# Feed-forward gate and up as seven half products in seven of 24 chunks

## The chip, the cores and the metric

The kernel runs on one core of a Trainium2 chip. The metric is the device time of one execution in microseconds (us); the median of three runs is compared.

## The reference, cut to what matters

x is 256 tokens of 1024. Two layers each do a feed-forward, a mixer (a gated recurrence and attention) and a second feed-forward. The change touches the feed-forwards alone:

```python
def swiglu_ffn(h, w_up, w_down):            # w_up: 1024 x 5632, w_down: 2816 x 1024
    gate, up = jnp.split(h @ w_up, 2, axis=-1)
    return (jax.nn.silu(gate) * up) @ w_down
for l in range(DEPTH):                      # DEPTH = 2
    x = x + 0.5 * swiglu_ffn(rms_norm(x, g_ffn1[l]), w_up1[l], w_down1[l])
    ...                                     # the mixer
    x = x + 0.5 * swiglu_ffn(rms_norm(x, g_ffn2[l]), w_up2[l], w_down2[l])
```

## The kernel before

Each float32 product is made of three matmuls in the format fp32r: an operand is split into a high part (a cast) and a low part (what the cast lost), and high x high, high x low and low x high are added in PSUM.

**Weights.** The unit is a half chunk ("hc"): two k tiles of 128 rows by 512 columns, 0.52 MB. `plan` lists all of them in the order of use. `emit_dma` (L299) issues the next load on SP, into one of four raw buffers; `emit_hi` casts it on ScalarE (L332), `emit_lo` subtracts on VectorE (L341), and then calls `emit_dma` for the load four places on. The high and low parts lie in rings of six (`RING`): `can_hi` allows a cast when the entry six places back has been used by both token halves (`NT` = 2).

**Products.** `visit` runs one hc for one token half of 128: two k tiles, three matmuls of 512 columns each (L398 to L400). `block` runs four hcs for token half 0, then the same four for half 1, into two PSUM banks of the pools x or z (z has four). In `ffn` a chunk is 512 of the 2816 hidden columns (the sixth has 256): a gate block, an up block, and then the down block of the chunk before (four hcs). `ev_g` makes silu on ScalarE (L635), `ev_u` multiplies on VectorE (L640), and `h_chain` turns the result: a copy (L316 or L319), a transpose by a DMA on SP (L515), a copy back, and a split (L500, L502).

**The order of work.** The class `Sched` keeps a clock for each engine with planned costs while the program is written out. After each k tile, `hook` steps the waiting chains and `split` casts and subtracts ahead. So each engine's order is fixed ahead of time, and an instruction that waits holds up what is behind it on its engine. Background chains are stepped only where their engine is planned less than 2.5 us behind (`SLACK`). `rows_chain` loads the small vectors early in the first feed-forward, transposes them later, and then makes tables of ones on ScalarE (L675). Twelve equal slots of SBUF are given out and back by `slot` and `free`.

Of the kernel before, what the change touches and what calls it, by code (L numbers as in the profile page):

```python
# [15 lines left out]
P = 128  # L16
# [31 lines left out]
WARM0 = 10  # L48
WARM1 = 8


# [104 lines left out]
def act_c(n, ap=0):  # L156
    return 0.11 + 0.000833 * n + 0.093 * ap
# [7 lines left out]
def hybrid_encoder_kernel(  # L165
# [72 lines left out]

    hcs = []

    def plan(w, r0, c0, nk, ncol):
        hcs.append((w[r0:r0 + nk * P, c0:c0 + ncol].rearrange("(k p) n -> p k n", p=P), nk, ncol))

# [16 lines left out]

    def plan_ffn(wu, wd):
        for c, (f0, n) in enumerate(CH):
            plan_block(wu, f0, n)
            plan_block(wu, FF + f0, n)
# [22 lines left out]
    for l in range(L):  # L287
        plan_ffn(w_up1[l], w_down1[l])
        plan_mix(l)
        plan_ffn(w_up2[l], w_down2[l])  # L290
    NHC = len(hcs)
# [7 lines left out]
    def emit_dma(cuts=1):  # L299
        i = nxt["dma"]  # L300
        if i >= NHC:
            return
        nxt["dma"] += 1
        src, nk, ncol = hcs[i]
# [4 lines left out]
        raws[i] = t  # L309

# [12 lines left out]
    def can_hi():  # L323
        i = nxt["hi"]
        return i < NHC and i in raws and (i < RING or used[i - RING] == NT)

    def emit_hi():
        i = nxt["hi"]
        nxt["hi"] += 1
        _, nk, ncol = hcs[i]  # L330
        hi = new(whi_p, [P, nk, ncol], "whi", F32R)
        nc.scalar.copy(hi, raws[i])  # L332
        his[i] = hi, S.use("a", act_c(1024))

    def emit_lo():
        i = nxt["lo"]
        nxt["lo"] += 1
        _, nk, ncol = hcs[i]
        hi, end = his.pop(i)
        lo = new(wlo_p, [P, nk, ncol], "wlo", F32R)  # L340
        nc.vector.tensor_tensor(out=lo, in0=raws.pop(i), in1=f32(hi), op=ALU.subtract)  # L341
        S.use("d", dve_c(1024), end)
        ready[i] = (hi, lo)
        emit_dma()

    def split(lead, idle):
        if nxt["pos"] < 3:
            lead = 1
        if can_hi() and nxt["hi"] - nxt["pos"] <= lead and (idle is None or S.busy("a") < idle):
# [8 lines left out]
    def first_split(xT, gcol):  # L358


        _, nk, ncol = hcs[0]
        raw = raws.pop(0)
        hi, lo = new(whi_p, [P, nk, ncol], "whi", F32R), new(wlo_p, [P, nk, ncol], "wlo", F32R)
# [18 lines left out]
    def get_hc(i):  # L382
        while nxt["lo"] <= i:
            if nxt["hi"] == nxt["lo"]:
                assert can_hi()
                emit_hi()
            emit_lo()
        nxt["pos"] = max(nxt["pos"], i)
        return ready[i]

    def visit(i, acc, lhs, k0, tok, first, last, fin=None):

        hi, lo = get_hc(i)
        _, nk, ncol = hcs[i]
        ts = slice(tok * P, tok * P + P)
        for kk in range(nk):
# [5 lines left out]
            if kk == nk - 1:  # L402
                used[i] += 1
                if used[i] == NT:
                    ready.pop(i)
                if fin is not None:
                    fin()
# [192 lines left out]

    def ffn(nrm, nxn, mixed=0):
        lhs = nrm.lhs()
# [12 lines left out]
        def down(c, tok, hf, i0, last):  # L615
# [5 lines left out]
            for i in range(m):  # L621
# [3 lines left out]
                visit(i0 + i, dacc[tok, hf], src, 2 * i, tok, c == 0 and i == 0, last and i == m - 1, fin)  # L625

        for c, (f0, n) in enumerate(CH):
            hT[c] = slot([P, 2, 4, T], F32R)
# [600 lines left out]
    def program():  # L1229
# [39 lines left out]
        for l in range(L):  # L1269
            nx = Norm(cols[:, l, R_GM:R_GM + KD])  # L1270
            if l:
                S.add(load_fw(l), S.now, "a")
            ffn(nrm, nx, 1 if l == 0 else 0)
# [6 lines left out]
            ffn(nrm, nx)  # L1280
            nrm = nx
# [31 lines left out]
```

## Time and profile before

| | |
|---|---|
| median of three runs | 1267.83 us (1267.33 to 1272.08) |
| the profiled execution | 1271.76 us, span 1270.0 us |
| granted TensorE clock, mean | 0.999 |
| busy share of the span | TensorE 99%, VectorE 65%, ScalarE 65%, GpSimd 5% |
| matmuls | 5889 |
| DMA | 253.50 MB, mean 200 GB/s |

The profile is of one execution; times in its rows are us from the first instruction of the span. A busy time counts an engine's instructions alone; matmuls overlap, so the spacing of their starts, and not their duration, says what one costs.

### The profile page before, as it was taken

Reading aid. Unit: us, or ns where it says so; the run is one execution under the profiler, and the core shown is the slowest. Engines: PE = TensorE matmul, PEld = TensorE weight load, DVE = VectorE, ACT = ScalarE, POOL = GpSimd, SP = SyncE. Lnnn points to the kernel's source line nnn. Section 1 sums busy time; section 2 is a strip of 40 time slices with the busy share of each in tenths; the row PEclk is TensorE's granted clock in tenths of the full one; section 3 lists DMA queues with packets and bytes.
Section 4 is the critical chain, followed back from the end, with each engine's and each line's share of the span. In section 5 each row is a group of like instructions: output and inputs, shape, how many; then the busy total and the mean of one; then the engine's idle time right before and its main releaser. Section 6 shows DMA issues by size and latency. Waiting matters only on the chain.

```text
span 1270.0 us, 16219 instructions
## 1 busy us (share of the span) xinstructions
PE 1255.3 (99%) x5889; PEld 1033.6 (81%) x5889; DVE 824.9 (65%) x1158; ACT 826.8 (65%) x1086; POOL 68.6 (5%) x88
## 2 busy tenths in 40 slices
PE   9999999999999999999999999999999999999998
PEld 7887887788877888888878888878887778888887
DVE  6655556798777666555475555578987767655553
ACT  6657556886799456555566555569768984665553
POOL 4000000001400000000000000000032000000000
PEclk9999999999999999999999999999999999999999
DMA  7977769576567568667768677596676665687773
GB/s 252 247 212 217 223 173 257 142 222 208 166 174 188 178 190 212 205 213 206 193 195 238 199 207 207 157 276 163 203 218 156 184 189 174 200 223 215 215 189 102
DMA packets 212304, 253.50 MB, mean 200 GB/s; under 512 B 92488, under 2 KB 104960, under 8 KB 212224
## 3 DMA queue, kind: packets, MB, share of 16 engines
q1 hardware_dynamic: 210288, 249.21, 67.8%
q0 software_dynamic: 1920, 3.26, 1.2%
q8 instruction: 46, 0.75, 0.3%
q14 instruction: 34, 0.28, 0.1%
q10 hardware_dynamic: 16, 0.00, 0.0%
HBM read 229.88 MB, written 2.10 MB: 183 GB/s over the span
## 4 chain that ended last, share of the span: by engine, by line
PE 72%; DVE 5%; DMA 2%; issue 1%; ACT 1%; SPq 0%; DVEq 0%; ACTq 0%
PE x L398 11%; PE x L400 11%; PE x L399 11%; PE z L398 9%; PE z L400 9%; PE z L399 9%; PE y L398 3%; PE y L400 3%; PE y L399 3%; DVE wlo L341 2%; PE z L1010 1%; PE z L479 1%; PE y L1082 1%; DMA tmp<-in_b_gate_dram 1%; PE z L820 1%
## 5 line engine op out<-in xcount | busy, mean ns | idle before, releaser
L341 DVE TENSOR_TENSOR wlo<-raw,whi 128x1024 fp32r<-128x1024 f32 x423 | 510.2, 1221 | 220.6 <-ACT whi L332 213.3
L332 ACT CAST whi<-raw 128x1024 fp32r<-128x1024 f32 x423 | 439.5, 1048 | 208.4 <-PE z L400 122.0
L398 PE MATMUL x<-whi,s 128*128 128x512 f32 x800 | 323.3, 404 | 5.5 <-ACT s L500 2.4
L399 PE MATMUL x<-wlo,s 128*128 128x512 f32 x800 | 312.9, 391 | 0.8 <-DVE wlo L341 0.7
L400 PE MATMUL x<-whi,s 128*128 128x512 f32 x800 | 313.3, 392 | 0.1
L398 PE MATMUL z<-whi,s 128*128 128x512 f32 (+1 forms) x752 | 279.6, 372 | 1.0 <-ACT s L500 1.0
L399 PE MATMUL z<-wlo,s 128*128 128x512 f32 (+1 forms) x752 | 279.8, 372 | 0.1
L400 PE MATMUL z<-whi,s 128*128 128x512 f32 (+1 forms) x752 | 279.6, 372 | 0.0
L398 PEld LDWEIGHTS x<-whi,s 128*128 128x128 f32 x800 | 150.4, 188 | 40.9 <-ACT s L500 4.7
L400 PEld LDWEIGHTS x<-whi,s 128*128 128x128 f32 x800 | 150.4, 188 | 34.9 <-DVE s L502 2.5
L399 PEld LDWEIGHTS x<-wlo,s 128*128 128x128 f32 x800 | 150.6, 188 | 30.9 <-DVE wlo L341 2.0
L399 PEld LDWEIGHTS z<-wlo,s 128*128 128x128 f32 x752 | 141.8, 189 | 26.0 <-DVE wlo L341 1.8
L398 PEld LDWEIGHTS z<-whi,s 128*128 128x128 f32 x752 | 141.8, 189 | 25.6 <-ACT s L500 1.4
L400 PEld LDWEIGHTS z<-whi,s 128*128 128x128 f32 x752 | 141.8, 189 | 25.0 <-DVE s L502 0.8
L319 ACT COPY tmp<-nat 128x1024 uint16<-128x1024 uint16 (+1 forms) x88 | 96.3, 1114 | 75.9 <-DMA nat<-tmp 67.9
L398 PE MATMUL y<-whi,s 128*128 128x512 f32 x208 | 82.4, 396 | 0.0
L400 PE MATMUL y<-whi,s 128*128 128x512 f32 x208 | 81.1, 390 | 0.0
L399 PE MATMUL y<-wlo,s 128*128 128x512 f32 x208 | 81.1, 390 | 0.0
L640 DVE SCALAR_TENSOR_TENSOR nat<-z,rstd,nat 128x512 f32<-128x512 f32 (+1 forms) x48 | 33.9, 705 | 56.3 <-PE z L400 56.3
L502 DVE TENSOR_TENSOR s<-tmp,s 128x512 fp32r<-128x512 f32 (+1 forms) x71 | 46.6, 656 | 34.8 <-ACT s L500 34.4
L500 ACT CAST s<-tmp 128x512 fp32r<-128x512 f32 (+1 forms) x71 | 42.1, 594 | 28.1 <-DVE tmp L529 26.5
L635 ACT ACTIVATE nat<-z,rstd 128x512 f32<-128x512 f32 (+1 forms) x46 | 29.9, 651 | 45.1 <-PE z L400 45.0
(164 smaller groups left out, 903.1 us busy)
## 6 DMA issues: line engine op xcount, KB each, us to landing
raw<-in_w_up_dram SPq DMA_DIRECT2D x175, 512.0 KB, 4.7
raw<-in_w_in_dram SPq DMA_DIRECT2D x112, 512.0 KB, 4.6
raw<-in_w_down_dram SPq DMA_DIRECT2D x88, 512.0 KB, 4.5
raw<-in_w_lru_out_dram SPq DMA_DIRECT2D x16, 512.0 KB, 5.0
raw<-in_w_attn_out_dram SPq DMA_DIRECT2D x16, 512.0 KB, 3.8
raw<-in_w_o_dram SPq DMA_DIRECT2D x16, 512.0 KB, 4.4
s<-ones_d POOLq DMA_DIRECT2D x16, 128.0 KB, 4.3
tmp<-in_b_gate_dram SPq DMA_DIRECT2D x8, 256.0 KB, 4.7
```

Source lines behind the costliest of these rows:

```text
L319: nc.scalar.copy(out_, in_)
L332: nc.scalar.copy(hi, raws[i])
L341: nc.vector.tensor_tensor(out=lo, in0=raws.pop(i), in1=f32(hi), op=ALU.subtract)
L398: nc.tensor.matmul(acc, lhsT=lhs(0, k0 + kk)[:, ts], rhs=hi[:, kk, :], start=st, stop=False)
L399: nc.tensor.matmul(acc, lhsT=lhs(0, k0 + kk)[:, ts], rhs=lo[:, kk, :], start=False, stop=False)
L400: nc.tensor.matmul(acc, lhsT=lhs(1, k0 + kk)[:, ts], rhs=hi[:, kk, :], start=False, stop=sp)
L479: nc.tensor.transpose(dst_ps[:, j * P:(j + 1) * P], src[:, j * P:(j + 1) * P], ident)
L500: nc.scalar.copy(hi, t)
L502: nc.vector.tensor_tensor(out=lo, in0=t, in1=f32(hi), op=ALU.subtract)
L635: nc.scalar.activation(s[tok][0], acc, AF.Silu, scale=rs(tok))
L640: nc.vector.scalar_tensor_tensor(out=h, in0=acc, scalar=rs(tok), in1=h, op0=ALU.mult, op1=ALU.mult)
L820: nc.tensor.matmul(ps[:, g, :], lhsT=wax[0][:, g, n, :], rhs=xr[0][:, n, :], start=True, stop=True)
```

## The change

Seven chunks (the fourth in the first feed-forward, the third and fifth in the other three) compute gate and up together as one product of 2 x 2 blocks: tokens in halves, the 1024 rows in halves of 512, and gate and up as the two column halves. Seven products of half blocks take the place of eight. Names: "11" and "12" are the upper rows of gate and up, "21" and "22" the lower ones; t1 to t4 are sums of these, made in place: t3 = 22 - 12, t1 = 12 - 11, t2 = t3 + 11, t4 = 21 - t2. A set is seven operands of two hcs each, used in the order 11, t1, t2, 21, t3, 22, t4, each hc once (`uses` 1) and not twice. Its eight loads go to five slots and not to raw buffers; they are placed in the list behind each of the eight ordinary loads ahead of the set, and a set's hcs trigger no loads. t3 and t1 are summed by a background chain planned 6 us after the last load, t2 and t4 when the low part of what they overwrite has been made. `sums_chain` makes three sums of the token halves once a feed-forward and splits them. In `seven` the products come into z banks and are joined by seven additions on VectorE and one copy on ScalarE; gate and up of token half 0 are made behind the fourth and sixth product, those of half 1 behind the last. The wait in `rows_chain` is 25 us and not 70.

```diff
+SEVEN = ((3,), (2, 4), (2, 4), (2, 4))
+    ORDER = ("11", "t1", "t2", "21", "t3", "22", "t4")
+    class Seven:
...
+        def load(self, name, u, src):
+            if not self.t:
+                for k in ("11", "12", "22", "21", "t3"):
+                    self.t[k] = slot([P, 4, 512])
+            nc.sync.dma_start(out=self.part(name, u), in_=src)
+            if name != "12":
+                raws[self.index(name, u)] = self.part(name, u), 0.0
+            if (name, u) == ("21", 1):
+                self.chain = S.add(self.sums(), S.now + 6.0, "d", True)
+        def sums(self):
+            def op(name, u, dst, a, b, f):
+                o = self.part(dst, u)
+                nc.vector.tensor_tensor(out=o, in0=self.part(a, u), in1=self.part(b, u), op=f)
+                raws[self.index(name, u)] = o, S.use("d", dve_c(1024))
+            for u in range(2):
+                op("t3", u, "t3", "22", "12", ALU.subtract)
+                yield S.now, "d"
+                op("t1", u, "12", "12", "11", ALU.subtract)
+                yield S.now, "d"
+            for name, dst, a, b, f in (("t2", "11", "t3", "11", ALU.add), ("t4", "21", "21", "11", ALU.subtract)):
+                for u in range(2):
+                    while nxt["lo"] <= self.index(dst, u):
+                        yield S.now + 0.5, "d"
+                    op(name, u, dst, a, b, f)
+                    yield S.now, "d"
...
+    def plan_seven(w, f0):
...
+        for name, r0, c0 in (("11", 0, f0), ("12", 0, FF + f0), ("22", 512, FF + f0), ("21", 512, f0)):
+            for u in range(2):
+                r = r0 + 256 * u
+                loads.insert(len(loads) - 7 + n, (w[r:r + 256, c0:c0 + 512].rearrange("(k p) n -> p k n", p=P),
+                                                       (st, name, u)))
+                n += 1
+        for _ in range(14):
+            hcs.append((2, 512))
+            uses.append(1)
...
     def emit_dma(cuts=1):
...
+        while loads and isinstance(loads[0][1], tuple):
+            src, (st, name, u) = loads.pop(0)
+            st.load(name, u, src)
...
-        return i < NHC and i in raws and (i < RING or used[i - RING] == NT)
+        return i < NHC and i in raws and (i < RING or used[i - RING] == uses[i - RING])
...
-        emit_dma()
+        if uses[i] == NT:
+            emit_dma()
...
+        def sums_chain():
...
+            for i, u, v, f in ((0, A(1, 0), A(1, 1), ALU.add), (1, B(0), A(0, 0), ALU.subtract),
+                               (2, A(0, 0), A(1, 0), ALU.subtract), (3, A(0, 1), B(1), ALU.subtract)):
+                yield S.now, "d"
+                nc.vector.tensor_tensor(out=B(i), in0=u, in1=v, op=f)
+                S.use("d", dve_c(512))
...
+        def seven(c):
...
+            def after_1(b, r):
+                nc.scalar.copy(s1, b)
...
+            def after_6(b, r):
+                plus(u2, b, s1)
+                r.free = True
+                plus(u4, b5[0], u2)
+            def after_2(b, r):
+                end = plus(s1, b, s1)
+                r.free = True
+                gate(0, s1, end)
+            def after_7(b, r):
+                plus(u2, b, u2)
+                r.free = True
+                plus(c22, b5[0], u2)
+                b5[1].free = True
+            def after_3(b, r):
+                end = plus(u4, b, u4)
+                r.free = True
+                up(0, u4, end)
+            def after_4(b, r):
+                end = plus(u2, b, u2)
+                r.free = True
+                up(1, c22, gate(1, u2, end))
+            prod("11", xh(0, 0), after_1)
+            prod("t1", xs(0), lambda b, r: b5.extend((b, r)))
+            prod("t2", xs(1), after_6)
+            prod("21", xh(0, 1), after_2)
+            prod("t3", xs(2), after_7)
+            prod("22", xs(3), after_3)
+            prod("t4", xh(1, 1), after_4)
...
-            block(lhs, ev_g, xbank if c < mixed else zbank, n, nrm if c == 0 else None, c < mixed)
-            block(lhs, ev_u, zbank, n)
+            if c in SEVEN[no]:
+                assert hpos[0] == sevens[0].i0
+                seven(c)
+            else:
+                block(lhs, ev_g, xbank if c < mixed else zbank, n, nrm if c == 0 else None, c < mixed)
+                block(lhs, ev_u, zbank, n)
...
-        yield S.now + 70.0, "p"
+        yield S.now + 25.0, "p"
```

## Rows read from the trace of the kernel before

**Rows 1.** The page's parts 1 and 5: busy time; groups (busy, mean ns, idle before).
```profile
PE 1255.3 (99%) x5889; PEld 1033.6 (81%) x5889; DVE 824.9 (65%) x1158; ACT 826.8 (65%) x1086; POOL 68.6 (5%) x88
...
L341 DVE TENSOR_TENSOR wlo<-raw,whi 128x1024 fp32r<-128x1024 f32 x423 | 510.2, 1221 | 220.6 <-ACT whi L332 213.3
```

**Rows 2.** Windows of a steady chunk: length, busy by engine, clock, DMA share, GB/s.
```profile
530.01:562.65 32.64, 32.64 (x145) 27.04 (x144) 17.74 (x17) 18.15 (x19) 0.00 (x0) 1.00 0.68 209
529.10:546.90 17.80, 17.80 (x80) 14.73 (x79) 9.88 (x10) 11.03 (x11) 0.00 (x0) 1.00 0.82 245
```

**Rows 3.** Timeline of TensorE: start, duration, the first matmul of two gate blocks.
```profile
513.49 0.39 PE L398 MATMUL z<-whi,s 128*128 128x512 f32 x1
...
546.13 0.39 PE L398 MATMUL z<-whi,s 128*128 128x512 f32 x1
```

**Rows 4.** Timeline of ScalarE in that chunk; in brackets idle time before and releaser.
```profile
534.09 1.05 ACT L332 CAST whi<-raw 128x1024 fp32r<-128x1024 f32 x1 [0.31 <-PE z L400]
...
544.81 1.35 ACT L319 COPY tmp<-nat 128x1024 uint16<-128x1024 uint16 x1 [2.72 <-DMA nat<-tmp]
546.04 1.04 ACT L332 CAST whi<-raw 128x1024 fp32r<-128x1024 f32 x1
```

**Rows 5.** Timeline of VectorE in that chunk.
```profile
521.58 3.94 DVE L341 TENSOR_TENSOR wlo<-raw,whi 128x1024 fp32r<-128x1024 f32 x3 [3.77 <-ACT whi L332]
...
536.12 2.35 DVE L341 TENSOR_TENSOR wlo<-raw,whi 128x1024 fp32r<-128x1024 f32 x2
540.66 1.22 DVE L341 TENSOR_TENSOR wlo<-raw,whi 128x1024 fp32r<-128x1024 f32 x1 [2.19 <-ACT whi L332]
...
542.41 1.22 DVE L341 TENSOR_TENSOR wlo<-raw,whi 128x1024 fp32r<-128x1024 f32 x1
547.11 1.23 DVE L341 TENSOR_TENSOR wlo<-raw,whi 128x1024 fp32r<-128x1024 f32 x1 [3.49 <-ACT whi L332]
548.25 0.69 DVE L502 TENSOR_TENSOR s<-tmp,s 128x512 fp32r<-128x512 f32 x1
548.85 1.22 DVE L341 TENSOR_TENSOR wlo<-raw,whi 128x1024 fp32r<-128x1024 f32 x1
```

**Rows 6.** Groups by line and form: count, busy us, mean ns, idle before.
```profile
L640 DVE SCALAR_TENSOR_TENSOR nat<-z,rstd,nat 128x512 f32<-128x512 f32 x40 | 30.0, 750 | 45.9 <-PE z L400 45.9
L635 ACT ACTIVATE nat<-z,rstd 128x512 f32<-128x512 f32 x38 | 26.2, 689 | 43.4 <-PE z L400 43.4
...
L1147 DVE TENSOR_TENSOR s<-x,s 128x512 f32<-128x512 f32 x8 | 5.5, 690 | 5.1 <-PE x L400 5.1
...
L885 DVE TENSOR_TENSOR s<-s,s 128x1024 f32<-128x1024 f32 x4 | 4.9, 1219 | 0.0
```

**Rows 7.** Window of a dense stretch of the first mixer.
```profile
270.00:310.00 40.00, 40.00 (x178) 33.09 (x177) 37.66 (x43) 28.57 (x32) 1.67 (x1) 1.00 0.67 205
```

**Rows 8.** Two windows with the DMA engines full, and the SP queue's total.
```profile
8.00:12.00 4.00, 3.94 (x21) 2.72 (x19) 2.65 (x5) 1.79 (x3) 0.00 (x0) 1.00 1.05 401
...
656.00:658.00 2.00, 2.00 (x10) 1.66 (x9) 1.23 (x1) 0.10 (x1) 0.00 (x0) 1.00 1.00 354
...
q1 hardware_dynamic: 210288, 249.21, 67.8%
```

**Rows 9.** Timeline of SP's queue: two transposes of h.
```profile
531.52 1.24 SPq L515 DMA_TRANSPOSE nat<-tmp  x1
...
538.92 1.24 SPq L515 DMA_TRANSPOSE nat<-tmp  x1
```

**Rows 10.** Windows behind the first mixer's end and behind the tables of ones.
```profile
640.00:660.00 20.00, 19.04 (x84) 14.88 (x83) 13.07 (x17) 10.14 (x16) 0.55 (x1) 1.00 0.79 249
110.00:120.00 10.00, 9.87 (x43) 7.43 (x42) 7.73 (x7) 7.66 (x9) 0.00 (x0) 1.00 0.81 256
```

**Rows 11.** Timelines of GpSimd (the last row load) and ScalarE (first tables of ones).
```profile
33.73 0.58 POOL L470 DMA_DIRECT2D bfb<-in_b_forget_dram  x1
...
99.38 3.16 ACT L675 COPY s<-ident 32x1024 f32<-32x1024 f32 x3
```

More of the change, by code (lines that the diff above doesn't have):

```diff
@@ L239, in hybrid_encoder_kernel, with __init__, index, part @@
     hcs = []
+    loads = []
+    uses = []
     def plan(w, r0, c0, nk, ncol):
-        hcs.append((w[r0:r0 + nk * P, c0:c0 + ncol].rearrange("(k p) n -> p k n", p=P), nk, ncol))
+        loads.append((w[r0:r0 + nk * P, c0:c0 + ncol].rearrange("(k p) n -> p k n", p=P), len(hcs)))
+        hcs.append((nk, ncol))
+        uses.append(NT)
+    ORDER = ("11", "t1", "t2", "21", "t3", "22", "t4")
+    class Seven:
+        def __init__(self):
+            self.i0 = len(hcs)
+            self.t, self.chain = {}, None
+        def index(self, name, u):
+            return self.i0 + 2 * ORDER.index(name) + u
+        def part(self, name, u):
+            return self.t[name][0][:, 2 * u:2 * u + 2]
+        def load(self, name, u, src):
[23 more added lines that the diff above has]
+                    yield S.now, "d"
+        def release(self):
+            for t in self.t.values():
+                free(t)
@@ L348, in split @@
             lead = 1
-        if can_hi() and nxt["hi"] - nxt["pos"] <= lead and (idle is None or S.busy("a") < idle):
+        if can_hi() and nxt["hi"] - nxt["pos"] <= lead and (
+                idle is None or S.busy("a") < idle) and raws[nxt["hi"]][1] <= max(S.now, S.t["a"]) + 0.05:
             emit_hi()
@@ L384, in get_hc @@
             if nxt["hi"] == nxt["lo"]:
+                for st in sevens:
+                    if st.i0 <= nxt["hi"] < st.i0 + 14:
+                        while nxt["hi"] not in raws:
+                            S.step(st.chain, True)
                 assert can_hi()
@@ L403, in visit @@
                 used[i] += 1
-                if used[i] == NT:
+                if used[i] == uses[i]:
                     ready.pop(i)
@@ L625, in down @@
                 visit(i0 + i, dacc[tok, hf], src, 2 * i, tok, c == 0 and i == 0, last and i == m - 1, fin)
+        sums = {}
+        def sums_chain():
+            for tok in range(NT):
+                for hf in range(2):
+                    yield nrm.done[tok, hf]
+            xh, xl = nrm.xT[0][0], nrm.xT[1][0]
+            a, b = slot([P, KD, T]), slot([P, 4, 4, P])
+            for q in range(2):
+                yield S.now, "d"
+                ks = slice(4 * q, 4 * q + 4)
+                nc.vector.tensor_tensor(out=a[0][:, ks], in0=f32(xh[:, ks]), in1=f32(xl[:, ks]), op=ALU.add)
+                S.use("d", dve_c(1024))
+            A = lambda tok, q: a[0][:, 4 * q:4 * q + 4, tok * P:(tok + 1) * P]
+            B = lambda i: b[0][:, i]
+            for i, u, v, f in ((0, A(1, 0), A(1, 1), ALU.add), (1, B(0), A(0, 0), ALU.subtract),
+                               (2, A(0, 0), A(1, 0), ALU.subtract), (3, A(0, 1), B(1), ALU.subtract)):
+                yield S.now, "d"
+                nc.vector.tensor_tensor(out=B(i), in0=u, in1=v, op=f)
+                S.use("d", dve_c(512))
+            free(a)
+            sums[0], sums[1] = slot([P, 4, 4, P], F32R), slot([P, 4, 4, P], F32R)
+            yield S.t["d"], "a"
+            for q in range(2):
+                ii = slice(2 * q, 2 * q + 2)
+                yield from split_seg(b[0][:, ii], sums[0][0][:, ii], sums[1][0][:, ii], 1024)
+                yield S.now, "a"
+            free(b)
@@ new lines, in ffn, with prod, plus, gate @@
+        sums_c = S.add(sums_chain(), S.now + 4.0, "d", True)
+        def seven(c):
+            st = sevens.pop(0)
+            S.need(sums_c)
+            xh = lambda tok, q: lambda e, k: nrm.xT[e][0][:, 4 * q + k, tok * P:(tok + 1) * P]
+            xs = lambda i: lambda e, k: sums[e][0][:, i, k, :]
+            w = slot([P, 4, 512])
+            s1, u2, u4, c22 = (w[0][:, i] for i in range(4))
+            h, b5 = {}, []
+            def prod(name, lhs_, fin):
+                b, r = zbank()
+                for u in range(2):
+                    visit(st.index(name, u), b, lhs_, 2 * u, None, u == 0, u == 1, (lambda: fin(b, r)) if u else None)
+            def plus(dst, x, y, dep=0.0):
+                nc.vector.tensor_tensor(out=dst, in0=x, in1=y, op=ALU.add)
+                return S.use("d", dve_c(512), dep)
+            def gate(tok, src, dep):
+                nrm.scaled(tok)
+                h[tok] = new_nat()
+                S.func("silu")
+                nc.scalar.activation(h[tok][0], src, AF.Silu, scale=rs(tok))
+                return S.use("a", act_c(512, 1), dep)
+            def up(tok, src, dep):
+                t, rh = h[tok]
+                nc.vector.scalar_tensor_tensor(out=t, in0=src, scalar=rs(tok), in1=t, op0=ALU.mult, op1=ALU.mult)
+                dep = S.use("d", dve_c(512), dep)
+                hch[c, tok] = rh.user = S.add(h_chain(c, tok, t, rh, dep), dep)
+            def after_1(b, r):
+                nc.scalar.copy(s1, b)
+                S.use("a", act_c(512))
+                r.free = True
[18 more added lines that the diff above has]
+                end = plus(u2, b, u2)
+                r.free = True
+                up(1, c22, gate(1, u2, end))
[6 more added lines that the diff above has]
+            prod("t4", xh(1, 1), after_4)
+            take(14)
+            st.release()
+            free(w)
+            if c == SEVEN[no][-1]:
+                free(sums[0])
+                free(sums[1])
```

50 lines of the change are left out of this document (28 added, 22 removed).

## The prediction

> **What bounds the kernel now.** I read the page's totals first, then the granted clock, then one steady chunk of a feed-forward, then who waits for whom in it. TensorE is busy 99% of the span, VectorE 65% [rows 1], and the clock stands at its upper level (1.00, so 2.4 GHz) in the chunk that I use [rows 2]. In that chunk the gate block begins at 513.49 us and the next one at 546.13 [rows 3]: 32.64 us for 144 matmuls of 512 columns, 0.2267 us each, with TensorE busy throughout. Nothing but the number of matmuls sets its length. VectorE works 17.74 us of it and ScalarE 18.15 [rows 2]. ScalarE's casts in it mostly wait for TensorE, which frees a ring entry every 1.36 us [rows 4], and VectorE's subtractions for the casts [rows 5]. So both helpers have room on average, and the question is whether they have it where the new work falls.
>
> **Fewer matmuls.** A gate and an up block are 2 x 2 x 4 x 2 x 3 = 96 matmuls; seven half products are 7 x 4 x 3 = 84. Twelve less at 0.2267 us [rows 3] is 2.72 us a set, and seven sets (one, two, two, two) give 19.0 us. This is the whole of the gain. The Trainium skill's page "VectorE: DVE Perf Modes", section "The TRN2 errata", gives a matmul max(60, 6 + columns) cycles, 0.216 us here. By that the gain would be 18.1 us; the measured spacing is 5% longer, and I go by it.
>
> **More splitting, sums and additions.** A set has 14 half chunks to split where there were 8: six more casts of 1.05 us on ScalarE [rows 4] and six more subtractions of 1.22 us on VectorE [rows 1]. The sums are eight additions of 1024 elements; the nearest row, an addition of that size, has 1.22 us [rows 6]. The products are joined by seven additions of 512 elements out of PSUM, like the product of a PSUM bank and SBUF that takes 0.69 us [rows 6], and one copy on ScalarE, of half the size of a cast. Back to back these VectorE operations follow each other closer: 547.11 to 548.25 is 1.14 us for the large, 548.25 to 548.85 is 0.60 for the small, and two large in a row take 2.35 [rows 5]. I take 1.16 and 0.61. VectorE's extra is (6 + 8) x 1.16 + 7 x 0.61 = 20.5 us a set; it had 32.64 - 17.74 = 14.9 us free in a chunk [rows 2]. So a set can't be paid out of its own chunk, only together with the one ahead.
>
> **What of it lies beside TensorE.** I set t = 0 at 546.13, where the set would begin. The ring holds six entries, so entry i can be cast when entry i - 6 has been used. Before the change an entry is used for 2.72 us, in a set for 1.36. Entries 0 to 3 are split before t = 0, as in the trace (536.12, two of them, 540.66, 542.41) [rows 5]; entry 4 is cast at 546.04 and ready for VectorE at about t = 0.8 [rows 4]. The set's last load is issued after the subtraction five entries ahead of the set, about t = -23 (the second of the three at 521.58 [rows 5]), and the chain of sums is planned 6 us later, t = -17: first t3 and t1, then, behind the subtractions of entries 0 and 1, t2. These six sums are 7.0 us. From t = -17 to 0.8 VectorE is busy 9.88 of 17.80 us [rows 2] and has 7.9 free: they just fit, and VectorE starts the set with nothing in hand.
>
> From t = 0.8 on VectorE must do, before the fourth entry of the following down block is wanted (19.04 us of set, and 5 x 1.36 us in the down block: t = 25.8): 10 + 4 subtractions and the two t4 sums, 16 x 1.16 = 18.6; seven additions, 4.3; the two multiplications by up, 1.4 (0.75 each [rows 6], some 0.7 back to back); a split of the h before, 0.6. Sum 24.9 us in 25.0. To this comes one wait: at the set's end token half 1 adds, ScalarE makes silu (0.69 [rows 6]), and VectorE, which stands in order, waits for it about 1 us; the down block's subtractions queue behind. So VectorE is short by 0.9 us if it never idles. It does idle a little: in a dense stretch of the mixer it is busy 37.66 of 40 us [rows 7], 94%. 24.9 / 0.94 + 1.0 is 27.5, short by 2.5 us. What VectorE is short TensorE waits, because each entry's low part is needed by its matmuls. The loss is 0.9 to 2.5 us a set.
>
> **The loads.** The bytes are the same, but eight set loads ride with the eight ordinary ones ahead, and SP then issues no more until the set is over. Twenty loads of 0.52 MB fall into about 34 us. Four us at the start move 401 GB/s with the engines full [rows 8], so a load takes 1.31 us of all of them: 26 us. The rest of the queue's 67.8% of the span [rows 8] must be the transposes of h: 861 us less 425 loads of 1.31 is 304 us over 76 transposes, 4.0 us each (my estimate). Two or three of them make 34 to 38 us. The queue is thus full to the brim, and the transposes at 531.52 and 538.92 [rows 9] land later than now. The one that matters is the second: ScalarE waits for it until 544.81, with the cast of entry 4 behind it [rows 4]. It can come 1.3 us late before t = 0 is passed; each us beyond that VectorE starts later and TensorE loses it. The ordinary loads have 4 to 5 us to spare and cost nothing. I put lateness at 0 to 1.3 us and take the loss of a set, all together, as 2.0 us of the 2.72.
>
> **The rest.** The three token sums (VectorE 2 x 1.16 + 4 x 0.61 + 2 x 1.16 = 7.1 us, ScalarE 2.1) come once a feed-forward, in its first 20 us, where VectorE is busy 13.07 of 20 us and TensorE already loses 0.96 [rows 10]. Room is there; I charge 0.25 us each, 1.0 in all (bounds: nothing, and that loss once more in each, 3.8). The rows' transposes and the ones move up by 45 us: the last row load is issued at 33.73 [rows 11], 11 us before the new place at about 45; ScalarE's eight copies in a burst (three take 3.16 us [rows 11]) go with them, after them TensorE lost 0.13 us [rows 10], and I expect no more there. I take it that the four z banks are handed out in the order in which they were given back (no row shows it); then 22 gets t2's bank, free since about t = 9, and nothing waits.
>
> **Sum.** 7 x (2.72 - 2.0) = 5.0 us gained, 1.0 lost: 4.0 less than the profiled run's 1271.76, which lies 3.9 above the median. On the median, 1264 us.
>
> **Rivals.** *VectorE keeps up.* In that dense stretch TensorE is busy 40.00 of 40 us [rows 7], so a full VectorE needn't stop it. Then a set loses 0.9 us and the token sums nothing: 7 x 1.82 = 12.7 less, 1255 us. Against it: those 40 us have entries used for 2.72 us, a set's only 1.36.
> *The transpose comes too late* (the other side). If the queue is 3 to 4 us behind at t = -7, ScalarE's copy ends at about t = 2 and the cast of entry 4 with it; the loss is 2.0 + 2.2 = 4.2 us a set, 7 x 1.5 + 1.0 = 11.4 more: 1279 us. It decides from 0.6 us more lateness than I take. For it: ScalarE waits for this landing already, 2.72 us [rows 4]; against it: the queue may take a burst faster than my 4.0 us a transpose.
> *The banks go in turn.* If 22 gets t1's bank, TensorE waits for two additions after t3's end, 1.2 us and the drain, refill and handovers of one matmul, 0.5: 1.7 us more a set, 1276 us. For it: four banks and the sixth product; against it, the order that I take.
> *Loads have a lower ceiling.* Two us of the second feed-forward move 354 GB/s with the engines full [rows 8]. If a burst of loads gets no more, a load takes 1.48 us, twenty take 3.4 us longer, and the transpose with them: a set loses 5.4 us, 7 x 2.7 + 1.0 = 20 more, 1288 us. Against it: the 401 of the same group, though only for 4 us. The Trainium skill's page "DMA: Bandwidth & Descriptors", section "Specifications", states about 358 GB/s as the limit of a core; the trace's 401 has passed it.
>
> **Chances.** My forecast 0.41 (a loss of 1.7 to 3.3 us a set: 1262 to 1273, within 0.5%); VectorE keeps up 0.34; the late transpose 0.16; banks in turn 0.06; the lower ceiling 0.03. Under 0.5%, 6.3 us, a measurement of this kernel says little. Faster 0.34, same 0.41, slower 0.25. For 8 in 10 the range runs from a loss of 0.5 us a set (1252) to the late transpose (1279).
>
> **What would show it.** Right: 84 matmuls fewer in the run's lines, in a set's 19 us TensorE pauses of 1 to 2 us, waiting for low parts from entry 10 on and at the start of the down block, with VectorE busy over 9 of 10 there. The silu wait on VectorE at the set's end, about 1 us. Wrong: pauses before t = 5 (loads or sums late), a pause between t3 and 22 (banks), ScalarE waiting for a transpose or a load past t = 0, or no pause at all. The prediction also fails if VectorE's order, which is fixed ahead of time, puts a sum whose load is missing in front of subtractions that are due.

## The result and the profile after

The changed kernel takes 1291.3 us (median of four runs, 1289.45 to 1294.46) against 1267.65 us before (four runs too) on the same chip: a ratio of 1.0181, 95% interval 1.0165 to 1.0196. It is slower by 23.6 us, and above the range. The profiled execution of it took 1294.46 us, span 1292.7 us; 22.7 us more than the profiled span before.

The page's parts 1 and 5 of the changed kernel, beside [rows 1] (groups: busy us, mean ns | idle before, releaser):

```profile
PE 1248.6 (97%) x5805; PEld 1014.2 (78%) x5805; DVE 987.5 (76%) x1336; ACT 869.8 (67%) x1144; POOL 70.1 (5%) x88
...
L416 DVE TENSOR_TENSOR wlo<-raw,whi 128x1024 fp32r<-128x1024 f32 x367 | 441.1, 1220 | 106.7 <-ACT whi L407 104.3
...
L481 PE MATMUL z<-wlo,s 128*128 128x512 f32 (+1 forms) x724 | 273.8, 378 | 18.3 <-DVE wlo L416 18.2
...
L279 DVE TENSOR_TENSOR s<-s,s 128x1024 f32<-128x1024 f32 x56 | 67.8, 1222 | 1.1
```

84 matmuls fewer are there, and VectorE is busy 162.6 us longer (987.5 - 824.9). TensorE stands idle for 18.3 us ahead of z matmuls that read a low part, released by VectorE.

To place the loss I took each block's length (first matmul to the next block's first) less its matmuls at 0.2267 us, after against before. The terms make up the 22.7 us (why the mixers got shorter, no run shows):

| part | us |
|---|---|
| matmuls saved, 84 x 0.2267 | -19.0 |
| pauses inside the seven sets (2.5, 4.7, 3.0, 1.0, 3.8, 4.7, 2.6) | +22.3 |
| the first down block behind each set, 0.92 to 0.98 | +6.6 |
| the chunk ahead of a set | +6.2 |
| starts of the first and third feed-forward | +7.1 |
| ends of the second and third feed-forward | +3.8 |
| mixers, tables of ones | -4.3 |

One set of the second feed-forward shows what the large terms are. Windows of the changed kernel from VectorE's wait ahead of the set to its start, and the set itself (length, busy by engine, clock, DMA share, GB/s):

```profile
501.39:516.20 14.81, 12.54 (x54) 9.74 (x53) 14.71 (x15) 9.51 (x11) 0.00 (x0) 1.00 0.65 190
516.20:539.92 23.72, 20.87 (x86) 15.22 (x84) 23.58 (x25) 16.86 (x19) 0.00 (x0) 1.00 0.11 22
```

84 matmuls need 19.04 us, this set takes 23.72, and VectorE is full throughout (23.58), as it was in the 15 us ahead (14.71). The timeline of TensorE in it:

```profile
527.34 0.50 PE L481 MATMUL z<-wlo,s 128*128 128x512 f32 x1 [0.72 <-DVE wlo L416]
...
529.74 0.50 PE L481 MATMUL z<-wlo,s 128*128 128x512 f32 x1 [0.72 <-DVE wlo L416]
...
532.19 0.50 PE L481 MATMUL z<-wlo,s 128*128 128x512 f32 x1 [0.80 <-DVE wlo L416]
...
542.31 0.50 PE L481 MATMUL x<-wlo,s 128*128 128x512 f32 x1 [0.64 <-DVE wlo L416]
```

Each pause waits for VectorE's low part, half chunk after half chunk, and costs the wait and some 0.3 us more around it. Why VectorE is late stands ahead of the set, in the timelines of SP, ScalarE and VectorE, one fence for each:

```profile
488.26 5.82 SPq L597 DMA_TRANSPOSE nat<-tmp  x1
494.18 0.53 SPq L380 DMA_DIRECT2D raw<-in_w_down_dram  x1
```
```profile
498.58 1.35 ACT L394 COPY tmp<-nat 128x1024 uint16<-128x1024 uint16 x1 [7.61 <-DMA nat<-tmp]
```
```profile
501.39 0.69 DVE L584 TENSOR_TENSOR s<-tmp,s 128x512 fp32r<-128x512 f32 x1 [9.16 <-ACT s L582]
501.99 2.35 DVE L416 TENSOR_TENSOR wlo<-raw,whi 128x1024 fp32r<-128x1024 f32 x2
504.26 3.61 DVE L279 TENSOR_TENSOR s<-s,s 128x1024 f32<-128x1024 f32 x3
```

A transpose stays 5.82 us at SP's head between the doubled loads. ScalarE, in order, waits 7.61 us for it, VectorE 9.16 us for ScalarE. The first sum starts at 504.26, 11.94 us ahead of the set, with the fixed order's other work behind it.

This is the wait of two sets, here and at the same place of the fourth feed-forward (6.71 us for a transpose); they lost most, 4.7 us each. Ahead of four others, the set of the first feed-forward and those in the fifth chunks (chunk 4 in the code), VectorE's last waits are for casts, and these wait for ordinary loads. Timelines of ScalarE and VectorE ahead of the second feed-forward's second set, and a window there:

```profile
570.57 1.05 ACT L407 CAST whi<-raw 128x1024 fp32r<-128x1024 f32 x1 [0.97 <-DMA raw<-in_w_down_dram]
573.12 1.05 ACT L407 CAST whi<-raw 128x1024 fp32r<-128x1024 f32 x1 [1.49 <-DMA raw<-in_w_down_dram]
```
```profile
571.65 1.23 DVE L416 TENSOR_TENSOR wlo<-raw,whi 128x1024 fp32r<-128x1024 f32 x1 [1.38 <-ACT whi L407]
572.80 3.62 DVE L279 TENSOR_TENSOR s<-s,s 128x1024 f32<-128x1024 f32 x3
```
```profile
563.30:578.20 14.90, 13.92 (x62) 11.20 (x61) 11.95 (x13) 7.45 (x9) 0.00 (x0) 1.00 1.06 404
```

The DMA engines are full at 404 GB/s, so a load lands about every 1.3 us, and every second one is a set's: the casts of ordinary ones start 2.55 us apart, and the first sum stands behind them, 12.87 us ahead of the set. Over the span, casts wait 83.5 us for loads of the feed-forwards' weights (11.6 before).

The third feed-forward's start lost most at one place. There VectorE waited 6.15 and 4.89 us for two transposes, and then TensorE (timeline) and the clock (window):

```profile
692.52 0.80 PE L481 MATMUL z<-wlo,s 128*128 128x512 f32 x1 [3.35 <-DVE wlo L416]
693.12 0.63 PE L482 MATMUL z<-whi,s 128*128 128x512 f32 x1
693.54 0.63 PE L480 MATMUL z<-whi,s 128*128 128x512 f32 x1
```
```profile
690.00:700.00 10.00, 7.48 (x21) 5.92 (x22) 9.94 (x11) 3.94 (x5) 0.00 (x0) 0.66 0.78 273
```

After a pause of 3.35 us the matmuls follow each other at 0.43 us and not 0.23, up to 698.24: the clock is at its lower level (1.2 GHz), which costs some 2.8 us more (my estimate, 13 spacings), a second price of the same wait.

### The profile page after: what moved, and what is told of

It reads as the page before. It is cut to its first block, busy times and chain, and to the rows that moved or that the text cites. A ratio compares the mean times of both kernels' runs of the same rounds, so it can differ in the third digit from the quotient of the medians.

```text
span 1292.7 us, 16279 instructions
## 1 busy us (share of the span) xinstructions
PE 1248.6 (97%) x5805; PEld 1014.2 (78%) x5805; DVE 987.5 (76%) x1336; ACT 869.8 (67%) x1144; POOL 70.1 (5%) x88
## 5 line engine op out<-in xcount | busy, mean ns | idle before, releaser
L416 DVE TENSOR_TENSOR wlo<-raw,whi 128x1024 fp32r<-128x1024 f32 x367 | 441.1, 1220 | 106.7 <-ACT whi L407 104.3
L407 ACT CAST whi<-raw 128x1024 fp32r<-128x1024 f32 x367 | 378.3, 1047 | 184.6 <-DMA raw<-in_w_up_dram 48.5
L481 PE MATMUL z<-wlo,s 128*128 128x512 f32 (+1 forms) x724 | 273.8, 378 | 18.3 <-DVE wlo L416 18.2
L480 PE MATMUL z<-whi,s 128*128 128x512 f32 (+1 forms) x724 | 269.7, 373 | 0.0
L482 PE MATMUL z<-whi,s 128*128 128x512 f32 (+1 forms) x724 | 269.6, 372 | 0.0
L481 PEld LDWEIGHTS z<-wlo,s 128*128 128x128 f32 x724 | 137.1, 189 | 55.4 <-DVE wlo L416 32.9
L480 PEld LDWEIGHTS z<-whi,s 128*128 128x128 f32 x724 | 137.1, 189 | 24.0
L482 PEld LDWEIGHTS z<-whi,s 128*128 128x128 f32 x724 | 137.2, 189 | 22.4
L416 DVE TENSOR_TENSOR wlo<-s,whi 128x1024 fp32r<-128x1024 f32 x98 | 116.6, 1217 | 0.5 <-ACT whi L407 0.5
L407 ACT CAST whi<-s 128x1024 fp32r<-128x1024 f32 x98 | 98.1, 1050 | 5.0 <-PE y L482 3.5
L279 DVE TENSOR_TENSOR s<-s,s 128x1024 f32<-128x1024 f32 x56 | 67.8, 1222 | 1.1
```

Source lines behind the costliest of these rows:

```text
L279: nc.vector.tensor_tensor(out=o, in0=self.part(a, u), in1=self.part(b, u), op=f)
L407: nc.scalar.copy(hi, raws[i][0])
L416: nc.vector.tensor_tensor(out=lo, in0=raws.pop(i)[0], in1=f32(hi), op=ALU.subtract)
L480: nc.tensor.matmul(acc, lhsT=lhs(0, k0 + kk)[:, ts], rhs=hi[:, kk, :], start=st, stop=False)
L481: nc.tensor.matmul(acc, lhsT=lhs(0, k0 + kk)[:, ts], rhs=lo[:, kk, :], start=False, stop=False)
L482: nc.tensor.matmul(acc, lhsT=lhs(1, k0 + kk)[:, ts], rhs=hi[:, kk, :], start=False, stop=sp)
```

## The experiments

Ratios are to the kernel before, run on the same chip (medians there 1267.7 to 1268.6 us).

**loads_alone.** The sets' loads go to their slots at the same places, but gate and up are computed as before: no sums, no additions, no token sums.

```diff
+            block(lhs, ev_g, xbank if c < mixed else zbank, n, nrm if c == 0 else None, c < mixed)
+            block(lhs, ev_u, zbank, n)
             if c in SEVEN[no]:
...
-                seven(c)
...
+                sevens.pop(0).release()
```

> The set's eight loads stay where the change puts them (into four slots, one behind each of the eight ordinary loads ahead), but gate and up are computed as before: 96 matmuls, eight half chunks, no sums, no additions. Theory Q (the loads crowd SP's queue, a transpose of h behind them lands 3 to 5 us later, ScalarE and VectorE stand in order behind it): the losses seen ahead of the sets and at the feed-forwards' starts and ends stay, 10 to 15 us, so 1278 to 1283 us, and landings of the transposes near 8 us. Theory V (VectorE hasn't the time for a set; the loads are harmless): within 3 us of 1267.7.

1268.51 us, ratio 1.000 (0.999 to 1.001). Its transposes land 5.5 us after issue (4.6 before), as late as in the changed kernel, and the time is theory V's: that costs nothing. Late transposes alone are not the cause. The loads themselves are less late here: casts wait 29.2 us for them (83.5 in the changed kernel). SP's next ordinary load waits for a subtraction there, so a late VectorE makes loads late too; how much of the 83.5 us that is, no run shows.

**no_weight_sums.** The eight sums of each set are left out; the late half products read unsummed matrices.

```diff
-                nc.vector.tensor_tensor(out=o, in0=self.part(a, u), in1=self.part(b, u), op=f)
-                raws[self.index(name, u)] = o, S.use("d", dve_c(1024))
+                raws[self.index(name, u)] = self.part("22" if dst == "t3" else dst, u), S.now
```

> The eight sums of weights are left out (each product takes a loaded half block in place of its sum); all loads, splits, products and additions stay. VectorE has 9.3 us less to do a set. Theory V: the pauses in the sets and behind them (4.1 us a set, 28.9 us in all) fall below 1 us a set: 1266 to 1270 us. Theory Q: VectorE still starts late behind the transposes and the chunk ahead still loses; 1275 to 1283 us.

1265.08 us, 0.9972 (0.9958 to 0.9985), 26 us less than with them, though the transposes land even later (6.2 us): a little under theory V's range. The sums cost 26 us, though VectorE's idle time over the span (305 us) is more than four times their 67.8 us. Four of the seven sets lose nothing now, the others 0.7 to 2.4 us, and 0.8 to 1.0 us stays at four of the seven down blocks behind. Even without its sums the change keeps only 3.6 of its 19.0 us.

**loads_by_gpsimd.** The sets' loads are issued by GpSimd, so that SP's queue has only the ordinary loads and the transposes.

```diff
-            nc.sync.dma_start(out=self.part(name, u), in_=src)
+            nc.gpsimd.dma_start(out=self.part(name, u), in_=src)
```

> The set's loads are issued by GpSimd's queue and no longer stand in SP's ahead of the transposes; nothing else changes. Theory Q: the transposes land within 5 to 6 us, the chunk ahead and the starts lose nothing (13 us back), VectorE starts the sums in time and a set loses about 2 us and not 4.1 (15 us back): 1262 to 1268 us. Theory V: only the chunk ahead and the starts come back, the set still loses 4 us: 1276 to 1282 us. If it is the DMA engines and not SP's queue that are full, about 1290.

1280.7 us, 1.0091 (1.0068 to 1.0114): 10.6 us back. The time is in theory V's range, but not by its mechanism: five sets now lose 1.04 to 1.14 us, where it expected 4 and theory Q 2. The sets in the third chunk (chunk 2) of the second and fourth feed-forward still lose 3.64 and 4.20; ahead of them ScalarE still waits 4.07 and 4.42 us for a transpose. The first feed-forward pays 5.40 us in its third chunk. VectorE's 1336 instructions stand in the same order as in the changed kernel, so what came back is lateness alone. With loads_alone this reads: lateness costs only where VectorE has nothing in hand, and VectorE's load costs more where something makes it start late.

**token_sums_later.** The token sums wait 26 us from the feed-forward's start, not for its input to be split.

```diff
-            for tok in range(NT):
-                for hf in range(2):
-                    yield nrm.done[tok, hf]
+            yield S.now + 26.0, "d"
...
-            st = sevens.pop(0)
+            st = sevens[0]
...
+            sevens.pop(0)
```

> The sums of the token halves are planned 26 us into a feed-forward and not 4. Theory S (these sums, 7 us of VectorE in the first 20 us, cause the losses at the starts of the first and third feed-forward, 2.5 and 4.7 us): 1284 to 1287 us. If the start of the first is theirs and that of the third is the late transposes: 1288 to 1290. If neither, 1291 or more, because they then fall into the loads' window.

1368.08 us, 1.0785 (1.0760 to 1.0809), far above the first two cases; the third ("1291 or more") holds it, but not for the reason given there. The edit changed much more than a place: VectorE's order was laid out anew, t4's sums went behind its other work, at 540.51 and 544.06 in a set that began at 521.9, and ScalarE's casts waited for them:

```profile
541.84 1.04 ACT L407 CAST whi<-s 128x1024 fp32r<-128x1024 f32 x1 [4.70 <-DVE s L279]
```

Sets lost up to 11.8 us. It tells nothing about the token sums, but that a set is ruined by where its sums stand in VectorE's order. no_token_sums asks the question directly.

**no_token_sums.** Token sums left out; their four half products read unsummed halves.

```diff
-        sums_c = S.add(sums_chain(), S.now + 4.0, "d", True)
...
-            S.need(sums_c)
...
-            xs = lambda i: lambda e, k: sums[e][0][:, i, k, :]
+            xs = lambda i: xh(i % 2, i // 2)
```

> The token sums of the four feed-forwards, and the split of them, are left out (the four half products that should read them read unsummed halves, so the output is not the reference's): 7.6 us of VectorE's work per feed-forward fewer. If they cost where they stand alone (1.74 us at the first feed-forward's start, part of 3.35 at the third's), 1286 to 1289 us. Rival: VectorE is so far behind from the feed-forward's start into the first set that each us taken from it comes back there: the sets in chunk 2 lose under 2 us instead of 4.7, 1.0 and 4.7, and the time is 1271 to 1282 us.

1285.76 us, 1.0138 (1.0111 to 1.0165): 5.5 us back, most of it at the starts of the first and third feed-forward (3.4 and 6.4 us less lost there, some lost elsewhere). The sets lose 22.9 us in sum, as before (22.3), though now 2.7 to 4.0 each. So the first theory holds (the time is just under its 1286): these 30 us of VectorE's work cost 5.5, and in sum nothing in the sets.

**sums_by_gpsimd** and **sums_and_loads_by_gpsimd.** The sums on GpSimd, without and with the loads.

```diff
-                nc.vector.tensor_tensor(out=o, in0=self.part(a, u), in1=self.part(b, u), op=f)
-                raws[self.index(name, u)] = o, S.use("d", dve_c(1024))
+                eng, e, cost = (nc.gpsimd, "g", 2.6) if name in GNAMES else (nc.vector, "d", dve_c(1024))
+                eng.tensor_tensor(out=o, in0=self.part(a, u), in1=self.part(b, u), op=f)
+                raws[self.index(name, u)] = o, S.use(e, cost)
```

`GNAMES` holds the names of all four sums; the planned cost of one on GpSimd is 2.6 us.

> The eight weight sums of each set run on GpSimd instead of VectorE; the loads stay on SyncE's queue. Theory V (VectorE has too little time in a set, whatever the queue does): VectorE has 8 x 1.22 = 9.8 us less to do in each set, as where the sums were left out (1265.1 us), so if GpSimd takes under about 3 us for one of them the time is 1264 to 1272 us and the set's pauses for low parts are gone. Rival G: GpSimd needs longer than the set gives it, or slows VectorE while it works; the low parts of the sums come late and the time is 1285 us or more, with the waits of the matmuls on parts made from sums.

> As before, and the loads of the sets are issued on GpSimd's queue too. If both causes are removed side by side (VectorE's 9.8 us a set, the transposes' lateness behind the loads), 1256 to 1264 us, faster than the kernel before. Rival: GpSimd issues the loads of a set behind the sums of the set ahead, in its order, so that the matrices land late: 1275 us or more, with waits of the casts on loads.

1327.68 us, 1.0472 (1.0454 to 1.0491), and 1329.31 us, 1.0485 (1.0458 to 1.0513). Both times lie where the rivals put them, and the first shows rival G's mechanism. The group of the sums in the first kernel, then its timelines of GpSimd and of VectorE ahead of a set, and a part of the view of VectorE's line from 498 to 540 us (min, median and max in ns):

```profile
L281 POOL TENSOR_TENSOR s<-s,s 128x1024 f32<-128x1024 f32 x56 | 182.2, 3268 | 293.7 <-DMA s<-in_w_up_dram 216.9 <-DVE wlo L418 75.7
```
```profile
498.82 10.04 POOL L281 TENSOR_TENSOR s<-s,s 128x1024 f32<-128x1024 f32 x4 [29.01 <-DMA s<-in_w_up_dram]
```
```profile
505.11 1.50 DVE L586 TENSOR_TENSOR s<-tmp,s 128x512 fp32r<-128x512 f32 x1 [8.13 <-ACT s L584]
506.54 4.54 DVE L418 TENSOR_TENSOR wlo<-raw,whi 128x1024 fp32r<-128x1024 f32 x2
```
```profile
L418 DVE TENSOR_TENSOR wlo<-raw,whi x4: 1211/1219/3408, 506.5 to 513.5; 128x1024 fp32r<-128x1024 f32 x4
```

A sum takes GpSimd 3.27 us on average (1.22 on VectorE), and VectorE's subtractions wait for it. Of the two in 4.54 us the first takes 3.41 and the second 1.21, as elsewhere: GpSimd's last sum ends at 508.86, the first subtraction at 509.94, 1.08 us later, as if it had begun only then. 26 subtractions of the span take over 2.2 us, and each ends 1.08 or 1.09 us after a sum's end. The wait shows as busy time: VectorE's is 1004.4 us, more than with the sums (987.5). Moving the work relieved it of nothing.

**no_sums_loads_by_gpsimd.** Both earlier edits.

> The eight weight sums are left out (the late half products use unsummed matrices, so the output is not the reference's) and the loads go by GpSimd's queue. What stays is the token sums and the additions behind the products. If the losses at the chunk ahead, the feed-forwards' starts and ends (17 us in the changed kernel) come from the loads' lateness, 1250 to 1256 us, near the saving of 19.0 us alone. Rival: they come from the token sums and the additions, which stay: 1260 to 1266 us, and the third feed-forward still starts 4 us late.

1267.6 us, 0.9996 (0.998 to 1.0012). No better than without the sums alone: no set loses anything there, but TensorE now waits 0.90 and 0.73 us for casts whose loads come late, the third feed-forward's start still loses 4.05 us (2.25 before the change), and two down blocks behind sets lose 2.0 us each. Moving the loads gave 10.6 us back with the sums and cost 2.5 without them: the two causes don't add. The rival's 1260 to 1266 lies nearer, though below the result.

**one_set_each.** One set a feed-forward, chunk 4 in all but the first.

```diff
-SEVEN = ((3,), (2, 4), (2, 4), (2, 4))
+SEVEN = ((3,), (4,), (4,), (4,))
```

> One set in each feed-forward (chunk 3 of the first, chunk 4 of the others) instead of two in three of them: four sets, 10.9 us of matmuls fewer. If each set costs the same wherever it stands (23.6 + 19.0 us over seven sets, 6.1 us each), 4 x 6.1 - 10.9 = 13.5 us slower than before, 1281 us. Rival: the cost comes from two sets close together (49 us apart) or the early one in chunk 2, near the feed-forward's start: the four left keep most of their saving, 1262 to 1270 us.

1269.52 us, 1.0014 (1.0004 to 1.0025), the rival's. The three sets of chunk 4 lose 1.04, 1.04 and 1.05 us; in the changed kernel, with a set 69 us before, the same chunks lost 3.0, 3.8 and 2.6. The fourth set, in the first feed-forward, is where it was and lost 4.10 (2.5 there). From the windows of one of them:

```profile
563.67:579.10 15.43, 15.43 (x69) 12.76 (x69) 14.96 (x15) 11.00 (x12) 0.00 (x0) 1.00 0.75 219
579.10:599.18 20.08, 19.48 (x85) 15.53 (x84) 19.34 (x21) 15.51 (x17) 0.00 (x0) 1.00 0.00 0
```

The first sum begins at 563.67, 15.43 us before the set. I call this the lead. Read from the timelines of all 35 sets of the changed kernel, loads_by_gpsimd, no_token_sums, one_set_each and the two kernels that come next:

| lead, us | 11.8 to 12.1 | 12.4 to 13.0 | 13.2 to 13.4 | 13.8 to 13.9 | 14.7 to 15.2 | 15.4 and more |
|---|---|---|---|---|---|---|
| sets | 8 | 8 | 4 | 2 | 2 | 11 |
| loss in the set, us | 3.8 to 4.7 | 3.0 to 4.2 | 2.5 to 2.7 | 1.9 to 2.0 | 1.2 to 1.3 | 1.04 to 1.14 |

About 1 us more is lost for each us less of lead, above a floor of 1.04 us; sets of nearly the same lead differ by up to 1.2 us. The third feed-forward's first set in the changed kernel is no exception: it lost only 1.04 us because TensorE had already lost 4.7 at the start (lead 17.0); without the token sums that start lost nothing, the lead was 12.7 and the set lost 3.0.

**low_before_up** and **one_late_set.** At the set's end a waiting low part of the down block is made ahead of the multiplication by up; the second kernel has that, one set in each of the last three feed-forwards and none in the first.

```diff
-                up(1, c22, gate(1, u2, end))
+                end = gate(1, u2, end)
+                S.split(RING + 1, None)
+                up(1, c22, end)
```

> One line put in: at a set's end VectorE makes a waiting low part of the next down block before it takes the up result's multiplication, which waits 0.79 us for silu. Theory: the 0.94 us that the matmuls lose at the down block behind every set is this wait, handed on; then those pauses fall under 0.35 us, worth 7 x 0.6 = 4 us: 1287 us. Rival: VectorE is behind by more than the wait anyway, and the pause only moves to the next low part: within 1 us of the changed kernel's 1291.

> One set only in the second, third and fourth feed-forward (chunk 4), none in the first, with the low part ahead of the up result. 3 x 2.72 = 8.2 us of matmuls fewer. One set alone lost 1.04 us in its block and 0.94 at the down block behind it; with the latter down to 0.3, 3 x 1.34 = 4.0 us are lost, and 1263 to 1266 us remain. Rival: the losses at the feed-forwards' ends (4.0 and 0.9 us with one set each) stay and eat the rest: 1267 to 1270 us, no gain.

1301.52 us, 1.027 (1.0244 to 1.0296), and 1278.36 us, 1.0092 (1.0061 to 1.0122). Neither time lies in a range that was named. The theory that silu's wait of 0.79 us makes the down block's pause fell: in the changed kernel the seven multiplications waited 5.6 us for it, here not at all, and the loss of 0.94 to 0.98 us there stays. VectorE's timeline of the first kernel shows what it is:

```profile
603.78 1.22 DVE L416 TENSOR_TENSOR wlo<-s,whi 128x1024 fp32r<-128x1024 f32 x1
604.91 1.22 DVE L416 TENSOR_TENSOR wlo<-raw,whi 128x1024 fp32r<-128x1024 f32 x1
606.04 0.68 DVE L757 TENSOR_TENSOR s<-z,s 128x512 f32<-128x512 f32 x1
606.76 0.75 DVE L769 SCALAR_TENSOR_TENSOR nat<-s,rstd,nat 128x512 f32<-128x512 f32 x1
607.43 2.35 DVE L416 TENSOR_TENSOR wlo<-raw,whi 128x1024 fp32r<-128x1024 f32 x2
```

The addition and the multiplication of token half *0* stand between the down block's first low part and its second, which begins at 607.43; the block's matmul waits for that until 608.71. The new loss is elsewhere: at the ends of the second and third feed-forward the down block lost 9.0 and 8.2 us (2.7 and 1.1 in the changed kernel), as the last chunk's transposes came late:

```profile
640.32 0.76 ACT L394 COPY tmp<-nat 128x512 uint16<-128x512 uint16 x1 [5.29 <-DMA nat<-tmp]
```

One row's place on VectorE had changed the order of what comes behind it: some 30 of VectorE's 1336 instructions and 11 of SP's 523 loads and transposes stand elsewhere in the order. The same ends cost one_late_set 8.9 and 6.5 us in its profiled execution (1286.13 us, the longest of five), and so it is 9 us slower than one_set_each with a set less.

**sums_started_earlier**, **earlier_sums_loads_by_gpsimd** and **one_late_set_both.** The chain of sums is handed to the order a matrix earlier; the second has the loads on GpSimd too, the third both with three late sets alone.

```diff
-            if (name, u) == ("21", 1):
+            if (name, u) == ("22", 1):
```

> The sums' chain is handed to the order when the third of the four matrices is loaded instead of the fourth, which puts VectorE's first sums about three low parts earlier in its order. Theory L (lead): over the 16 sets of the changed kernel, loads_by_gpsimd and one_set_each, a set loses 1.04 us where VectorE began its first sum 15.4 us or more before the set, and about 1 us more for each us less of it (2.5 at 13.3, 3.0 at 12.9, 4.7 at 11.9). Then leads of 15 us or more bring all seven sets to 1.04 to 1.5 us: 22.3 - 9 = 13 us faster than the changed kernel, 1276 to 1281 us. Rival: VectorE's whole work ahead of the set decides, and its order does not: the low parts put behind the sums come late instead, pauses move into the chunk ahead, and the time is 1288 us or more.

> Both: the sums earlier in VectorE's order and the sets' loads on GpSimd's queue. By theory L only the two sets that still lost 3.6 and 4.2 us with the loads on GpSimd's queue gain, 5 to 6 us: 1274 to 1276 us, and the remaining 1.04 + 0.94 us a set stays. Rival (queue): the loads by GpSimd had taken all that can be had, 1279 to 1282 us.

> One set in the second, third and fourth feed-forward, sums earlier, loads by GpSimd, up result as in the changed kernel. By theory L 3 x (2.72 - 1.98) = 2.2 us are won at the sets, less what the token sums and the feed-forwards' ends cost (1 to 3 us where the transposes come in time): 1265 to 1269 us, no version beats the kernel before by its measurement. Rival: with the transposes in time nothing else is lost: 1263 to 1265 us.

1319.38 us, 1.0406 (1.0363 to 1.0449); 1292.34 us, 1.019 (1.015 to 1.023); 1273.22 us, 1.004 (1.0013 to 1.0067). The first is the rival's, the other two lie above both of their ranges. Theory L was half right. Leads in the first two are now 21 to 31 us and no set there loses more than 0.27 us; even the floor of 1.04 is gone. But the time of the first is 28 us worse. Timelines of VectorE and of TensorE in the chunk ahead of one set, and its windows:

```profile
573.87 2.48 DVE L279 TENSOR_TENSOR s<-s,s 128x1024 f32<-128x1024 f32 x2 [2.04 <-DMA s<-in_w_up_dram]
576.27 2.35 DVE L416 TENSOR_TENSOR wlo<-raw,whi 128x1024 fp32r<-128x1024 f32 x2
```
```profile
577.55 0.79 PE L481 MATMUL z<-wlo,s 128*128 128x512 f32 x1 [5.21 <-DVE wlo L416]
```
```profile
573.87:597.80 23.93, 20.25 (x78) 16.48 (x78) 20.41 (x20) 12.26 (x13) 0.00 (x0) 0.86 0.71 233
597.80:617.08 19.28, 19.28 (x86) 15.69 (x84) 19.01 (x20) 14.69 (x16) 0.00 (x0) 1.00 0.00 0
```

The sums now wait for their matrices (2.04 here, up to 5.71 us), the low parts behind them wait too, TensorE pauses up to 6.5 us at one place, and the clock falls again (0.86). Chunks ahead of sets lost 5.6 to 9.2 us, the starts of the last three feed-forwards 3.0 to 6.9 more than before the change, the ends of the second and third 7.3 and 5.4 more. So no place for the sums was free: later, the set loses; earlier, VectorE stands before matrices that are not there yet. With the loads on GpSimd's queue the earlier order costs 11.6 us against loads_by_gpsimd. The three late sets come within half a per cent of the kernel before, not below it; no version that computes all of it was faster.

## Why the prediction was wrong

**Matmuls.** Right: 84 fewer, 19.0 us.

**VectorE's balance from t = 0.8.** Right in its items: VectorE does just the work listed there in the second set of one_set_each. Its sum, "short by 0.9 us if it never idles", taken as 2.0 in all, is near too: the three sets of one_set_each, which had the lead, lost 1.04 + 0.94 = 1.98 us each. That the size agrees so well is luck in part: the 0.9 was silu's wait, and that wait (0.8 us) cost nothing; the loss stood ahead of it. The form was right: pauses for low parts (from the ninth entry on, not the eleventh), VectorE over 9 of 10, and no pause for a bank between t3 and 22.

**The step that failed** is its starting point: that the chain of sums begins at t = -17 and its six sums "just fit" into 7.9 us that VectorE has free by then. In the changed kernel it began at -11.9 to -13.4 in six of seven sets. Free time of VectorE was not time at its disposal: it stood waiting, in order, for ScalarE, and ScalarE for a transpose (two sets) or for ordinary loads (four). I put lateness at 0 to 1.3 us, from the transposes of a chunk in which no doubled loads were yet under way [rows 9], and looked only at the one that holds entry 4's cast [rows 4]. It is the transpose of the chunk ahead that holds the sums, or the loads behind it. The measured loss was 3.18 in the set and 0.94 behind it, 4.1 us, and not 2.0: 14.9 us over seven sets. That is the size that the rival "the transpose comes too late" had (4.2 us a set), through another wait than the one it named; that the sizes agree is luck.

**The loads.** "The ordinary loads have 4 to 5 us to spare and cost nothing" holds for loads_alone (1.000; casts waited 29.2 us for loads, 83.5 in the changed kernel), and fails together with the sums: casts waited for them ahead of four sets, and loads_by_gpsimd, in which the four lose 1.04 to 1.14 us, gave 10.6 us back in all. I had added the two causes; they don't add, as the slack that hides one is what the other uses up.

**The token sums and the rest**, charged 1.0 us, were mis-sized: the token sums cost 5.5 us (no_token_sums). I think that is because the window of a feed-forward's first 20 us [rows 10] shows a busy share and not the instruction that VectorE stands at; no run shows the reason. The chunk ahead of a set, and the feed-forwards' ends, had no term at all (6.2 and 3.8 us). The sets' 14.9, the starts' 7.1 less the 1.0 charged, these two, and the 4.3 that the mixers and the tables gave back make up the 26.7 us between the forecast for the profiled run, 1267.76, and the 1294.46 measured.

**What stays open.** In the first feed-forward's set and the three in chunk 4 the late start is the loads' lateness: loads_by_gpsimd, with VectorE's order the same, brought them to 1.04 to 1.14 us. Whether full DMA engines or late issues make the loads late was not taken apart (SP's next load waits for a subtraction), nor what holds the transpose in the two sets that gained little. The shorter wait in `rows_chain` was never run alone. A version in which the set's loads come earlier as well as its sums was not tried.

## What to carry to other kernels

Where a change spends a helper's free time, ask what the helper stands at in that time: idle time behind an in-order wait can't be spent, and a late transfer that cost nothing becomes a loss as soon as its slack has a second user. Price work by the window between its input's landing and its first use, not by busy shares. In a program whose order is fixed ahead, try an edit's removal before its move: taking work out gave clear answers here, moving one row re-ordered what stands behind it and cost 10 to 77 us.

## What the hardware showed

GpSimd's two-operand sums and VectorE's two-operand subtractions took turns: a subtraction of 1.22 us that met a sum took up to 3.44 us and ended 1.08 us after the sum, shown as busy throughout, so an idle GpSimd was no help for a full VectorE. The Trainium skill's page "Trainium Architecture — The Big Picture", section "What this means for kernel authors", says that VectorE and GpSimd share a pair of ports under an exclusive lock; this trace agrees: all 26 subtractions of over 2.2 us end 1.08 or 1.09 us after a sum.

TensorE's clock fell to its lower level at single pauses of 3.35 us (granted clock 0.66 over 10 us) and 5.21 us (0.86 over 24 us); pauses of 0.6 to 0.8 us, four in one set, left it at 1.00.

The DMA engines, full, moved 404 GB/s over 14.9 us.
